# Preparations of passes one to three among the second pass's first products, and logits' products in pairs

## The chip, the cores and the metric

The kernel runs on one core of one Trainium2 chip. The metric is the device time of one execution in microseconds. Three runs of the kernel before took 724.37, 722.12 and 724.14 us, a median of 724.14. Each core has a matrix engine (TensorE, PE in the profile, its weight loads PEld), VectorE (DVE), ScalarE (ACT), GpSimd (POOL), and a sequencer (SP) that here issues most of the transfers. Each engine runs its own instructions in the order in which they were laid down.

## The reference, cut to what matters

One decoder layer on 512 tokens of width 1024: token mixing (attention and gated DeltaNet branches), whose merged result `m` goes through an output projection, and then a mixture of 32 experts in 4 groups of 8.

```python
h = rms_norm(x, norm1_w) * (1 + sc1) + sh1
x = x + g1 * (m @ w_out)                        # output projection
h = rms_norm(x, norm2_w) * (1 + sc2) + sh2
pg = softmax(h @ w_rg + b_rg)                   # group logits: 4
le = (h @ w_re + b_re).reshape(T, 4, 8)         # expert logits: 32
# the best group, in it the best 2 experts; comb = their weights
for e in range(32):
    a = silu(h @ w_gate[e]) * (h @ w_up[e])     # 1024 -> 256, twice
    y = y + (a * comb[:, e]) @ w_down[e]        # 256 -> 1024
out = rms_norm(x + g2 * y, final_norm_w)
```

Every token goes through two experts only. All data are float32.

## The kernel before, in words

**The output projection** (`project_out`, from about 413 us). The 1024 output features stand in 8 blocks of 128, features on the partitions, the 512 tokens along the row. Block i takes 24 matrix products, three for each of 8 slices k (`mm3`, lines 138 to 140: float32 split into a high and a low part). VectorE then adds the gated sum to the residual stream (line 1058, `x1 = blk(i)`). While the blocks run, the 36 routing logits (32 experts, 4 groups) are summed up too: two blocks at a time, behind blocks 1, 3 and 5, two products (line 1078) with 64 weight columns each, the even block into output partitions 0 to 63 of one accumulator bank, the odd one into 64 to 127. Four transposes for each block (`rows`, line 1050) turn the finished blocks to token rows, ScalarE copies these back (line 1051), and the first half of the rows is stored to DRAM (`xd`) by a transfer that ScalarE issues (line 1090); the second half follows behind the projection. ScalarE and VectorE split the next block's weights meanwhile (lines 143, 144).

**The experts** (`moe`, from about 477 us). 13 passes handle 128 token places each: passes 0 to 9 hold two experts (64 and 64 places, or 96 and 32), passes 10 to 12 four experts of 32. Passes 0 to 2 hold six experts that are fixed beforehand; for the later ones VectorE ranks the experts by their token counts, so their weights can be asked for only when that order is known. A pass needs these steps:

- `match(p)`: VectorE compares the tokens' positions with a counter and so makes the one-hot table of tokens by places (line 1645).
- `places(p)`: 12 tiny products on TensorE turn the table into the token numbers (`idx`) and a scale of each place. `weights(p)`: 4 tiny products more for the routing weights of the places (lines 1702, 1704). From pass 3 on `places` does both.
- `fetch(p)`: GpSimd issues an indirect transfer that gathers the 128 rows from `xd` (line 1683).
- `scale(p)`: ScalarE scales the left half of the rows, VectorE the right half (lines 1708, 1709).
- `features(p, b)`: four transposes (line 1718) of half b; ScalarE (b = 0, line 1722) or VectorE (b = 1, line 1725) copies them, modulated, into `xe`. Pass 0 has another way (`first_rows`): products with a one-hot table straight from the blocks, and no gather.
- `up(p)`: 8 blocks k of products of `xe` with the gate and up weights (line 1796), each expert in its own group of output partitions; then silu (line 1818), `gate` on VectorE (line 1823), `turn` (two transposes, line 1831, and ScalarE's copy, line 1832), and `down(p)` (line 1847), which VectorE and ScalarE evacuate (lines 1858 to 1861).
- `add(n)`: 8 pairs of products scatter the pass's result back to the token rows, one pass later (lines 1870 to 1872).

**The order.** `step` ties the first TensorE and SP instructions of a part behind the last ones of the part before, so on TensorE and SP the written order holds. What isn't tied is placed by a planner with its own costs. `tc.issue_after(x)` adds such a tie: instructions inside the block come behind x on x's engine, without a wait between engines. `between` of `up` is called ahead of each block k: in pass 0 `first_steps` puts the work on the routing there: at k = 0 the features of pass 0 and places and gathers of passes 1 and 2, at k = 2 the ranks of the tokens and the tables of routing weights, at k = 4 `match(0)` and `places(0)`, at k = 7 `weights(0)`. Behind `up(0)` stand `scale(1)`, `gate(0)`, `features(1, 0)`, `features(1, 1)`, `turn(0)` and `down(0)`, one load, and then `weights(1)`, `weights(2)`, `match(3)`, `places(3)` and `fetch(3)`, before `up(1)` begins.

**The weights' stream.** The experts' weights, 96 units of 1 MB (two for up and one for down of each expert), go through a ring of 18 tiles. SP asks for the next units behind blocks 3 and 7 of `up` and behind `down` (`load`, line 1005), each request waiting until the products that read the tile before are done.

The code around the change, with the lines of the profile:

Of the kernel before, what the change touches and what calls it, by code (L numbers as in the profile page):

```python
# [34 lines left out]
NP = len(PASSES)  # L35
# [22 lines left out]
def rows(p):  # L58
    o = 0
    for g, (q, n) in enumerate(p):  # L60
        yield g, q, slice(o, o + n)
        o += n
# [31 lines left out]
class Prog:  # L94
# [912 lines left out]
    def project_out(self):  # L1007
# [3 lines left out]
        with tc.tile_pool(name="ps_out", bufs=1, space=PSUM, reuse_waits="tile") as pp:  # L1011
# [34 lines left out]
            def rows(i):  # L1046

                p = pp.tile([128, 4, 128], F32, name="tr", bufs=2)
                for t in range(4):
                    nc.tensor.transpose(p[:, t], blk(i)[:, t], self.ident)  # L1050
                nc.scalar.activation(blk(i), p, AF.Copy)
            for i in range(7):
                wh, wl = self.unit_w(None, self.wo[i])
                ps = pp.tile([128, 512], F32, name="pj", bufs=2)
                for k in range(8):
                    self.mm3(ps, wh[:, k], wl[:, k], self.mhi[:, k], self.mlo[:, k], k == 0, k == 7)
                x1 = blk(i)
                v.scalar_tensor_tensor(x1, tiles(ps), self.mod[:, 16 + i:17 + i], x1, op0=OP.mult, op1=OP.add)
                if i == 0:
                    nc.scalar.activation(asq, x1, AF.Square)  # L1060
                else:
                    s2 = tiles(pp.tile([128, 512], F32, name="tr", bufs=2))
                    nc.scalar.activation(s2, x1, AF.Square)
                    v.tensor_add(asq, asq, s2)
                if i == 0:
                    with tc.issue_after(self.un_dma.ins):
                        nc.sync.dma_start(self.acc[:, :, 512:], I["xA"][:, :, 512:])
                        for j in (6, 7):
                            self.wo.append(self.uraw[j % 2])
                            self.un_dma = nc.sync.dma_start(self.wo[j], I["w_out"][:, j])  # L1070
                    with tc.issue_after(self.un_dma.ins):
                        self.load(12)
                elif i in (1, 3, 5):
                    self.load(1)
                if i in (1, 3, 5):

                    for g in range(2):
                        mm(tiles(lt[64 * g:64 * g + 64]), w6[:, i - 1 + g], blk(i - 1 + g), start=i == 1, stop=i == 5)
                    if i == 5:
                        nc.scalar.activation(lT, tiles(lt), AF.Copy)  # L1080
                elif i == 6:
                    pr[0] = pp.tile([128, 512], F32, name="rt0")[:, 0:36]
                    for t in range(4):
                        mm(pr[t], lT[:, t], sel, start=True, stop=False)
                        mm(pr[t], x1[:, t], self.wr[:, 6], start=False, stop=False)
                if i in (1, 3):
                    rows(i - 1)
                    rows(i)
                if i == 3:
                    nc.scalar.dma_start(xv[:, :, 0:512], self.acc[:, :, 0:512])  # L1090
                if i == 6:
                    psq = pp.tile([128, 512], F32, name="tr", bufs=2)
                    for t in range(4):
                        sums(psq[:, t:t + 1], asq, t)
                    v.tensor_scalar(ss, psq[:, 0:4], 1.0 / D, EPS, op0=OP.mult, op1=OP.add)
# [262 lines left out]
    def moe(self, es):  # L1358
# [32 lines left out]
        for p in range(NP):  # L1391
            if 0 < p < NP - 1:
                with ExitStack() as late:
                    for x in self.after_down:
                        late.enter_context(tc.issue_after(x))
                    self.scale(p + 1)
            if 0 < p < NP - 3:
                self.match(p + 3)
            if p == NP - 1:
                self.step(self.finish_init)  # L1400
                with ExitStack() as late:
                    for x in self.after_down:
                        late.enter_context(tc.issue_after(x))
                    self.step(self.alike, p)
            self.up(p, between=self.first_steps if p == 0 else None)
            if p == 0:
                with tc.issue_after(self.at_tables):
                    self.scale(1)
            self.gate(p)
            if p + 1 < NP:  # L1410
                self.step(self.features, p + 1, 0)
                if p == 0:
                    self.step(self.features, 1, 1)
            else:
                self.step(self.gather, 1)
            if p:
# [29 lines left out]
                    self.step(self.finish_last, h)  # L1446
                self.store_last(p)
            self.step(self.load, len(PASSES[p]) - (p == 0))
            if p == 0:
                for i in (1, 2):  # L1450
                    self.step(self.weights, i)
                self.match(3)
                self.step(self.places, 3)
                self.fetch(3)
        self.last = {}
        self.rest()

# [301 lines left out]
    def first_steps(self, k):  # L1759
# [12 lines left out]
        elif k == 2:  # L1772
            self.step(self.by_rank)
            self.tables()

            with self.tc.issue_after(self.at_exp):
                self.nc.scalar.activation(self.nt2[:, 0:1], self.ones[:, 0:1], AF.Silu)
        elif k == 4:
            self.match(0)
            self.step(self.places, 0)  # L1780
        elif k == 7:
            self.step(self.weights, 0)

    def up(self, p, experts=None, part=None, between=None):

# [150 lines left out]
```

## Time and profile before

| what | value |
|---|---|
| profiled execution, device time | 724.38 us |
| its span, first to last instruction | 722.5 us |
| TensorE busy | 692.8 us (96%) |
| VectorE busy | 485.5 us (67%) |
| ScalarE busy | 283.0 us (39%) |
| experts' weights into tiles `ra`, `rb`: median from issue to landing | 10.6 and 10.7 us |
| mean granted TensorE clock | 0.993 of full |

A busy TensorE isn't TensorE at its peak, as products are pipelined and their ends are modelled; starts are to be trusted more than durations. The granted clock is the share of full speed that the chip let TensorE have in a stretch. The DMA share is the mean busy share of the core's 16 DMA engines. In the rows on the timeline a number in brackets is the time that the engine stood idle before the instruction, and the arrow names what ended the wait. Lines L138 to L1872 are lines of the kernel.

### The profile page before, as it was taken

The numbers are of one execution on the slowest core, as the hardware profiler recorded it, in microseconds if no ns is written. First come the engines' busy times: TensorE is split into PE (matmuls) and PEld (weight loads), VectorE is DVE, ScalarE is ACT, GpSimd is POOL, SyncE is SP. The second block draws the span as 40 slices with busy tenths as digits, with TensorE's granted clock in tenths as the row PEclk, the third lists the DMA queues.
The fourth block names the chain that finished last, engine by engine and source line by source line (L and its number), as shares of the span: only waits on it lengthen the run. The fifth ranks groups of instructions, "written<-read, shape, count | busy, mean of one in ns | idle before, by whom it ended". The sixth has DMA issues, their size and how long they took to land. (4 is left out here: it accounts for less than half of the span.)

```text
span 722.5 us, 10988 instructions
## 1 busy us (share of the span) xinstructions
PE 692.8 (96%) x3939; PEld 481.7 (67%) x3939; DVE 485.5 (67%) x1243; ACT 283.0 (39%) x554; POOL 36.1 (5%) x43
## 2 busy tenths in 40 slices
PE   7999999999999899999999999998899999999995
PEld 5887868878798777876778867793444444554531
DVE  6987669968447677578766744284577766777654
ACT  5745357652233224367652323143122222322352
POOL 0002000520000000000000000100000000000000
PEclk9999999999999999999999999999999999999998
DMA  9942221058765772361168998068799999999994
GB/s 357 394 168 69 97 85 62 30 149 295 215 235 191 250 251 89 120 232 60 44 215 282 340 422 354 2 237 322 277 351 418 418 415 404 419 417 418 427 418 190
DMA packets 47756, 183.12 MB, mean 253 GB/s; under 512 B 11786, under 2 KB 12330, under 8 KB 34514
## 3 DMA queue, kind: packets, MB, share of 16 engines
q1 hardware_dynamic: 40930, 169.65, 62.3%
q10 hardware_dynamic: 4896, 8.51, 3.3%
q0 software_dynamic: 1872, 4.23, 1.6%
q8 instruction: 32, 0.52, 0.3%
q14 instruction: 26, 0.21, 0.1%
HBM read 175.63 MB, written 9.33 MB: 256 GB/s over the span
## 5 line engine op out<-in xcount | busy, mean ns | idle before, releaser
L138 PE MATMUL pj<-hR,uR 128*128 128x512 f32 x304 | 122.3, 402 | 1.5 <-DVE qk L762 1.5
L140 PE MATMUL pj<-hR,uS 128*128 128x512 f32 x304 | 122.1, 402 | 0.0
L139 PE MATMUL pj<-hR,uR 128*128 128x512 f32 x304 | 122.0, 401 | 0.0
L143 ACT ACTIVATE uR<-uF 128x1024 fp32r<-128x1024 f32 x48 | 50.8, 1060 | 104.1 <-PE pj L139 97.3
L1796 PE MATMUL gu<-ra,uS 128*64 128x512 f32 (+1 forms) x368 | 85.0, 604 | 1.4 <-DMA ra<-w_e 1.4
L144 DVE TENSOR_TENSOR uS<-uF,uR 128x1024 fp32r<-128x1024 f32 x48 | 58.4, 1219 | 25.8 <-ACT uR L143 24.1
L138 PEld LDWEIGHTS pj<-hR,uR 128*128 128x128 f32 x304 | 57.3, 188 | 14.2 <-issue 1.9
L140 PEld LDWEIGHTS pj<-hR,uS 128*128 128x128 f32 x304 | 57.3, 188 | 12.5 <-DVE uS L144 0.4
L139 PEld LDWEIGHTS pj<-hR,uR 128*128 128x128 f32 x304 | 57.3, 188 | 11.9 <-issue 0.3
L1872 DVE TENSOR_TENSOR accF<-accF,cb 128x512 f32<-128x512 f32 x96 | 59.7, 680 | 6.3 <-PE cb L1871 5.4
L219 DVE SCALAR_TENSOR_TENSOR sgF<-sgF,misc 128x1024 f32<-128x1024 f32 x32 | 38.9, 1218 | 12.7 <-DMA sgF<-w_mod 12.7
L1796 PEld LDWEIGHTS gu<-ra,uS 128*64 128x64 f32 (+1 forms) x368 | 25.0, 125 | 32.5 <-issue 27.8
L1823 DVE SCALAR_TENSOR_TENSOR uS<-uS,meta,gu 128x256 f32<-128x256 f32 x13 | 6.2, 480 | 55.1 <-ACT uS L1818 55.1
L1860 ACT ACTIVATE uR<-p2F 128x512 fp32r<-128x512 f32 x24 | 15.1, 632 | 67.2 <-DVE p2F L1858 63.3
L1870 PE MATMUL cb<-uR,oht 128*128 128x512 f32 x96 | 40.0, 416 | 0.0
L1871 PE MATMUL cb<-uR,oht 128*128 128x512 f32 x96 | 37.9, 395 | 0.0
L1796 PE MATMUL gu<-rb,uS 128*32 128x512 f32 (+1 forms) x136 | 32.5, 593 | 0.0
L1818 ACT ACTIVATE uS<-gu 128x256 f32<-128x256 f32 x13 | 5.0, 384 | 64.9 <-PE gu L1796 64.9
L138 PE MATMUL pj<-mR,uR 128*128 128x512 f32 (+1 forms) x72 | 27.3, 379 | 0.0
L409 DVE SCALAR_TENSOR_TENSOR dF<-dF,c_cols 128x512 f32<-128x512 f32 x36 | 26.6, 748 | 0.9
L139 PE MATMUL pj<-mR,uR 128*128 128x512 f32 (+1 forms) x72 | 27.0, 375 | 0.0
L140 PE MATMUL pj<-mR,uS 128*128 128x512 f32 (+1 forms) x72 | 26.8, 372 | 0.0
(437 smaller groups left out, 1346.0 us busy)
## 6 DMA issues: line engine op xcount, KB each, us to landing
ra<-w_e SPq DMA_DIRECT2D x54, 1024.0 KB, 10.6
rb<-w_e SPq DMA_DIRECT2D x25, 1024.0 KB, 10.7
uF<-w_in SPq DMA_DIRECT2D x38, 512.0 KB, 3.3
sgF<-w_mod SPq DMA_DIRECT2D x32, 512.0 KB, 4.8
rc<-w_e SPq DMA_DIRECT2D x15, 1024.0 KB, 8.1
sF<-w_mod SPq DMA_DIRECT2D x8, 1024.0 KB, 9.0
gd<-sgF ACTq DMA_DIRECT2D x16, 256.0 KB, 2.8
gF<-gd SPq DMA_DIRECT2D x8, 512.0 KB, 4.5
```

The source lines that it names most:

```text
L138: mm(ps, whi, xhi, start=first, stop=False)
L139: mm(ps, whi, xlo, start=False, stop=False)
L140: mm(ps, wlo, xhi, start=False, stop=last)
L143: self.nc.scalar.activation(hi, raw, AF.Copy)
L144: self.nc.vector.tensor_sub(lo, raw, hi.bitcast(F32))
L219: self.nc.vector.scalar_tensor_tensor(raw, raw, 1.0, self.cact, op0=OP.mult, op1=OP.mult, accum_out=self.mod[:, ot:ot + 1])
L409: nc.vector.scalar_tensor_tensor(a, r[:, k:k + 512], w[:, k:k + 1], a, op0=OP.mult, op1=OP.add)
L1796: nc.tensor.matmul(gu[r], xe[:, k, r], w[:, k % 4], start=k == 0, stop=k == 7)
L1860: i1 = nc.scalar.activation(self.yhi[:, c], self.yf[:, c], AF.Copy)
L1870: nc.tensor.matmul(pc, self.oht[:, ts], self.yhi[:, c], start=True, stop=False)
L1871: nc.tensor.matmul(pc, self.oht[:, ts], self.ylo[:, c], start=False, stop=True)
L1872: nc.vector.tensor_add(self.acc[:, t, c], self.acc[:, t, c], pc)
```

## The change

In the projection, the two logits' products of a pair, the transposes of the two blocks, and behind the last pair the copy of the logits, now stand in a helper `pair`. It is called inside blocks 2, 4 and 6, ahead of slice k = 2, and ties the two products one behind the other and behind the products of slice 1, and those of slice 2 behind both. In the experts, `weights(0)` moves from k = 7 to k = 4 of `up(0)`; `scale(1)` and `features(1, 0)` move from behind `up(0)` to its k = 6; `weights(1)`, `weights(2)` and `match(3)` move from the end of pass 0 to k = 3 of `up(1)`, `places(3)` and `fetch(3)` to its k = 5, and `match(4)` from ahead of `up(1)` to behind `fetch(3)`.

```diff
@@ -1049,11 +1049,29 @@
                 for t in range(4):
                     nc.tensor.transpose(p[:, t], blk(i)[:, t], self.ident)
                 nc.scalar.activation(blk(i), p, AF.Copy)
+            def pair(i):
+
+                w = next(x for x in reversed(nc.cur_bb.bb.instructions) if x.engine == mybir.EngineType.PE)
+                for g in range(2):
+                    with tc.issue_after(w):
+                        w = mm(tiles(lt[64 * g:64 * g + 64]), w6[:, i + g], blk(i + g), start=i == 0, stop=i == 4).ins
+                if i == 4:
+                    nc.scalar.activation(lT, tiles(lt), AF.Copy)
+                else:
+                    with tc.issue_after(w):
+                        rows(i)
+                        rows(i + 1)
+                    if i == 2:
+                        nc.scalar.dma_start(xv[:, :, 0:512], self.acc[:, :, 0:512])
+                return w
             for i in range(7):
                 wh, wl = self.unit_w(None, self.wo[i])
                 ps = pp.tile([128, 512], F32, name="pj", bufs=2)
                 for k in range(8):
-                    self.mm3(ps, wh[:, k], wl[:, k], self.mhi[:, k], self.mlo[:, k], k == 0, k == 7)
+                    with ExitStack() as es:
+                        if k == 2 and i in (2, 4, 6):
+                            es.enter_context(tc.issue_after(pair(i - 2)))
+                        self.mm3(ps, wh[:, k], wl[:, k], self.mhi[:, k], self.mlo[:, k], k == 0, k == 7)
                 x1 = blk(i)
                 v.scalar_tensor_tensor(x1, tiles(ps), self.mod[:, 16 + i:17 + i], x1, op0=OP.mult, op1=OP.add)
                 if i == 0:
@@ -1072,22 +1090,11 @@
                         self.load(12)
                 elif i in (1, 3, 5):
                     self.load(1)
-                if i in (1, 3, 5):
-
-                    for g in range(2):
-                        mm(tiles(lt[64 * g:64 * g + 64]), w6[:, i - 1 + g], blk(i - 1 + g), start=i == 1, stop=i == 5)
-                    if i == 5:
-                        nc.scalar.activation(lT, tiles(lt), AF.Copy)
-                elif i == 6:
+                if i == 6:
                     pr[0] = pp.tile([128, 512], F32, name="rt0")[:, 0:36]
                     for t in range(4):
                         mm(pr[t], lT[:, t], sel, start=True, stop=False)
                         mm(pr[t], x1[:, t], self.wr[:, 6], start=False, stop=False)
-                if i in (1, 3):
-                    rows(i - 1)
-                    rows(i)
-                if i == 3:
-                    nc.scalar.dma_start(xv[:, :, 0:512], self.acc[:, :, 0:512])
                 if i == 6:
                     psq = pp.tile([128, 512], F32, name="tr", bufs=2)
                     for t in range(4):
@@ -1394,7 +1401,7 @@
                     for x in self.after_down:
                         late.enter_context(tc.issue_after(x))
                     self.scale(p + 1)
-            if 0 < p < NP - 3:
+            if 1 < p < NP - 3:
                 self.match(p + 3)
             if p == NP - 1:
                 self.step(self.finish_init)
@@ -1402,15 +1409,10 @@
                     for x in self.after_down:
                         late.enter_context(tc.issue_after(x))
                     self.step(self.alike, p)
-            self.up(p, between=self.first_steps if p == 0 else None)
-            if p == 0:
-                with tc.issue_after(self.at_tables):
-                    self.scale(1)
+            self.up(p, between=self.first_steps if p == 0 else self.second_steps if p == 1 else None)
             self.gate(p)
             if p + 1 < NP:
-                self.step(self.features, p + 1, 0)
-                if p == 0:
-                    self.step(self.features, 1, 1)
+                self.step(self.features, p + 1, int(p == 0))
             else:
                 self.step(self.gather, 1)
             if p:
@@ -1446,12 +1448,6 @@
                     self.step(self.finish_last, h)
                 self.store_last(p)
             self.step(self.load, len(PASSES[p]) - (p == 0))
-            if p == 0:
-                for i in (1, 2):
-                    self.step(self.weights, i)
-                self.match(3)
-                self.step(self.places, 3)
-                self.fetch(3)
         self.last = {}
         self.rest()
 
@@ -1778,8 +1774,22 @@
         elif k == 4:
             self.match(0)
             self.step(self.places, 0)
-        elif k == 7:
             self.step(self.weights, 0)
+        elif k == 6:
+            with self.tc.issue_after(self.at_tables):
+                self.scale(1)
+            self.step(self.features, 1, 0)
+
+    def second_steps(self, k):
+
+        if k == 3:
+            for i in (1, 2):
+                self.step(self.weights, i)
+            self.match(3)
+        elif k == 5:
+            self.step(self.places, 3)
+            self.fetch(3)
+            self.match(4)
 
     def up(self, p, experts=None, part=None, between=None):
 
```

## Rows read from the trace of the kernel before

**Rows 1.** The page's first part: busy time, share of the span and number of instructions of each engine.

```profile
PE 692.8 (96%) x3939; PEld 481.7 (67%) x3939; DVE 485.5 (67%) x1243; ACT 283.0 (39%) x554; POOL 36.1 (5%) x43
```

**Rows 2.** Busy time by stretch of the expert passes: the stretch from and to (us), its length, then busy time and number of instructions of PE, PEld, DVE, ACT and POOL, the granted TensorE clock, the DMA share and GB/s.

```profile
493.00:500.00 7.00, 6.04 (x40) 2.46 (x38) 3.43 (x11) 2.84 (x7) 0.00 (x0) 1.00 0.80 302
500.00:507.00 7.00, 3.94 (x24) 1.32 (x24) 3.81 (x11) 1.92 (x4) 0.00 (x0) 1.00 1.00 358
507.00:513.00 6.00, 5.75 (x34) 2.15 (x36) 2.48 (x10) 0.00 (x0) 0.99 (x1) 0.72 0.52 173
513.00:520.00 7.00, 7.00 (x54) 3.88 (x51) 2.78 (x7) 1.97 (x6) 0.00 (x0) 1.00 0.84 286
520.00:527.00 7.00, 6.00 (x30) 3.06 (x30) 6.92 (x31) 0.31 (x1) 0.99 (x1) 1.00 0.92 365
527.00:534.00 7.00, 7.00 (x35) 2.71 (x32) 3.28 (x6) 2.02 (x4) 0.00 (x0) 1.00 0.83 286
534.00:640.00 106.00, 106.00 (x704) 50.97 (x704) 76.39 (x177) 28.52 (x63) 6.92 (x7) 1.00 1.01 416
```

**Rows 3.** TensorE's timeline (start, duration, engine, line, operation, out<-in, shape, count): the turn of pass 2, the turn of pass 11, and, in up of the last pass, the fourth expert's first product.

```profile
536.49 0.42 PE L1831 MATMUL gu<-ct,uS 128*128 128x128 f32 x2
...
679.76 0.38 PE L1831 MATMUL gu<-ct,uS 128*128 128x128 f32 x2
...
688.71 0.62 PE L1796 MATMUL gu<-ra,uS 128*32 128x512 f32 x1 [1.42 <-DMA ra<-w_e]
```

**Rows 4.** TensorE's timeline around the first pair of logits' products, at the start of block 2 of the projection.

```profile
425.39 0.40 PE L139 MATMUL pj<-mR,uR 128*128 128x512 f32 x1
425.63 0.40 PE L140 MATMUL pj<-mR,uS 128*128 128x512 f32 x1
425.95 1.07 PE L1078 MATMUL rt<-accF,oF 128*64 128x512 f32 x2
426.96 0.50 PE L138 MATMUL pj<-mR,uR 128*128 128x512 f32 x1
427.39 1.07 PE L1078 MATMUL rt<-accF,oF 128*64 128x512 f32 x2
428.39 0.66 PE L1050 MATMUL tr<-ct,accF 128*128 128x128 f32 x4
```

**Rows 5.** TensorE's timeline over down of pass 0, first and last products, and the weights' products behind them.

```profile
500.10 0.64 PE L1847 MATMUL cb<-uR,uS 128*64 128x512 f32 x1 [1.06 <-ACT uS L1832]
500.10 0.64 PE L1847 MATMUL cb<-ra,uS 128*64 128x512 f32 x1
500.58 0.59 PE L1847 MATMUL cb<-uR,uS 128*64 128x512 f32 x1
...
503.15 0.59 PE L1847 MATMUL cb<-uR,uS 128*64 128x512 f32 x1
...
503.68 0.35 PE L1702 MATMUL tr<-p2F,uS 128*128 128x6 bf16 x8
```

**Rows 6.** VectorE's timeline: the sum of block 1 of the projection.

```profile
426.06 0.75 DVE L1058 SCALAR_TENSOR_TENSOR accF<-pj,mod,accF 128x512 f32<-128x512 f32 x1 [3.46 <-PE pj L140]
```

**Rows 7.** TensorE's timeline from block 7 of up of pass 0 to the end of up of pass 1 (down of pass 0 left out).

```profile
496.50 1.08 PE L1796 MATMUL gu<-ra,uS 128*64 128x512 f32 x4
497.51 1.09 PE L1718 MATMUL tr<-ct,uF 128*128 128x128 f32 x8
498.60 0.44 PE L1831 MATMUL gu<-ct,uS 128*128 128x128 f32 x2
...
507.25 0.35 PE L1670 MATMUL tr<-MC,uS 128*128 128x1 bf16 x8 [3.22 <-DVE uS L1645]
...
507.74 5.35 PE L1796 MATMUL gu<-ra,uS 128*64 128x512 f32 x16
512.92 3.60 PE L1796 MATMUL gu<-rb,uS 128*64 128x512 f32 x16
516.46 0.65 PE L1718 MATMUL tr<-ct,uF 128*128 128x128 f32 x4
```

**Rows 8.** The timelines of VectorE and of ScalarE from the tables of routing weights to the match of pass 3.

```profile
489.85 0.28 DVE L1325 CAST p2F<-p2F 128x128 bf16<-128x128 f32 x1
...
493.12 0.72 ACT L1708 ACTIVATE uF<-uF,meta 128x512 f32<-128x512 f32 x1 [3.24 <-DMA uF<-xd,idx]
...
499.65 0.40 ACT L1832 ACTIVATE uS<-gu 128x256 f32<-128x256 f32 x1
...
498.64 1.37 DVE L1725 TENSOR_SCALAR uS<-tr,A,mod 128x128 f32<-128x128 f32 x4
...
505.21 0.69 DVE L1861 TENSOR_TENSOR uR<-p2F,uR 128x512 fp32r<-128x512 f32 x1
505.92 0.51 DVE L1704 TENSOR_REDUCE meta<-tr 64x1 f32<-64x3 f32 x3
506.44 0.76 DVE L1645 TENSOR_TENSOR uS<-ct,p2F 128x384 bf16<-128x384 f32 x2
```

**Rows 9.** SP's timeline: the requests behind block 3 of up of pass 1 and behind down of pass 1; and of the line that issues the gathers, the time from issue to landing of all twelve.

```profile
513.12 1.50 SPq L1005 DMA_DIRECT2D ra<-w_e  x2
...
526.91 1.59 SPq L1005 DMA_DIRECT2D rb<-w_e  x2
...
DMA to landing us min/median/max: 3.9/7.7/8.2
```

## The prediction

> **What bounds the kernel now.** The page's first part shows TensorE busy for 96% of the span [rows 1]; since a busy share can hide a wait for weights, the second view is the table of stretches over the expert passes [rows 2]. It shows two limits side by side: from 534 to 640 us TensorE is busy in all of 106.00 us, and the DMA engines are at share 1.01 with 416 GB/s. The transposes of the gated activations (L1831) of passes 2 and 11 start at 536.49 and 679.76, so nine passes take 143.27 us, 15.92 each, with no gap on TensorE. The last pass then waits 1.42 us for its weights [rows 3]. So TensorE's order sets the passes' pace, freed ring tiles set when weights may be asked for, and the stream of weights is never idle after 534; the end moves earlier by what TensorE gains before that, if the stream loses idle time too. It has idle time to lose: (1 - share) times length over the stretches from 493 to 534 gives 1.4 + 0 + 2.9 + 1.1 + 0.6 + 1.2 = 7.2 us [rows 2]. The chain of waits on the page ends in the last store and says nothing here. What the change can win is therefore read from TensorE's timeline: the output projection [rows 4] and the step from pass 0 to pass 1 [rows 7].
>
> **Part 1, the pairs of logits' products.** Ordinary output products start 0.23 us apart (425.39, 425.63). Then a logits' product of block 0 starts at 425.95, one output product (L138) at 426.96, the logits' product of block 1 at 427.39, and the transposes at 428.39 [rows 4]: 1.00, 0.43 and 1.00, in all 2.44 us. These logits' products fill 64 output columns each, one the lower and one the upper half, like the experts' products of two experts. The down products of pass 0 show what such neighbours cost: both start at 500.10, the second passes at 500.58, and from the last two (503.15) to the next work is 0.53 [rows 5]. Two of them together take 0.48 + 0.53 = 1.01 us, as long as one takes here alone, because the two halves run at once. The pair so costs 1.01 and the displaced output product its ordinary 0.23: 2.44 - 1.24 = 1.20 us saved, and 3 pairs give 3.6 us. TensorE has no gap between the ordinary products around it, so this is all on the path.
>
> Bounds: if the halves did not overlap, each would keep its 1.00 and only the broken-in product's extra 0.20 would go: 0.6 us for three. A loss needs the new fixed place to come before the block's sum is ready: VectorE writes it from 426.06 to 426.81 [rows 6], and the pair is due behind six products of the block that starts about 425.86, at 427.3, so 0.5 us of slack; the same cadence holds for the later pairs. Above, 1.3 per pair. I take 3.6, as rows 5 are the same tile shape and row length. The transposes to rows, their copies, the copy of the logits and the first store keep their number; they come 1.4 us later in a block of 5.6, and ScalarE, which issues that store, is not waited for there. Everything behind the projection hangs on TensorE's products, so the 3.6 us carry to the passes.
>
> **Part 2, from pass 0 to pass 1.** Now down of pass 0 ends at 503.68, small weights' products follow, TensorE waits 3.22 us for VectorE's match of pass 3, runs the places at 507.25, and needs 507.74 to 512.92 = 5.18 us for the first four blocks of pass 1's up products and 512.92 to 516.46 = 3.54 for the other four [rows 7]. The granted clock was 0.72 in that stretch against 1.00 before and after [rows 2]: full speed lost for part of it, after the gap; that cost 5.18 - 3.54 = 1.64. From 503.68 to 516.46 are 12.78 us. After the change pass 1's blocks follow down directly and the preparations stand among them: 2 x 3.54 = 7.08; weights' products 0.35 [rows 5]; places 507.25 to 507.74 = 0.49; and four more changes between 64-column and full products at 0.10 each, 0.40: the last step of down took 0.53 where a block of 3.54 / 4 = 0.885 is two ordinary steps of 0.44. Sum 8.32, gain 4.46.
>
> The match is hidden only if VectorE is done with it before block 5. VectorE ends down's evacuation at 505.90; the weights' products stand behind block 2, at about 503.9 + 3 x 0.885 = 506.5; four reductions (three took 0.51 at 505.92, so 0.7) and the match (0.76 at 506.44) give 508.0 [rows 8]; the places are due at 506.5 + 0.45 + 1.77 = 508.7. Cover 0.7 us; if it is missed, TensorE waits the difference, at most the 3.22 of today, and blocks 5 to 7 and the loads behind them wait with it. The match of pass 4 comes behind it on VectorE, which then stands nearly idle until the gate. Bounds of part 2: 4.46 - 1.64 if the clock still falls, 1.2 if also half of today's wait stays, and 5.0 if the changes of shape cost nothing and a little of the 1.06 us before down goes.
>
> The Trainium skill, "TensorEngine Tiling (Array Packing)", section Key Properties, speaks against this part: changing the tiling mode drains the engine, and the change puts full-width work between 64-column products at two new places. No page price is needed: by the rows that is the 0.40 already in the sum, and without it the gain would be 4.86.
>
> **Part 3, the tail of pass 0.** Four of the eight feature transposes (1.09 for eight, so 0.54) move in front of block 6, with two changes of shape (0.2): up ends 0.74 later. They need ScalarE's scaling, which waited for the gathered rows until 493.12 and was done at 493.84 [rows 8]; block 6 starts about 496.50 - 0.88 = 495.6 [rows 7], a cover of 1.8 us. ScalarE's four feature copies are then done under blocks 6 and 7, so the copy at 499.65, which stood behind them, can follow the turn (498.60, 0.44 long) at once: 0.55 won. Net loss 0.2; up to 0.34 more (a quarter of the 1.37 at 498.64) if VectorE takes a feature in front of the gate. The weights of pass 0, three blocks earlier, need tables done at 490.13 [rows 8], well before block 4. The two loads behind block 7 come 0.7 later, while 1.4 us of DMA idle time lies around them.
>
> **Queues.** On SP the two loads now at 513.12 follow block 3 of pass 1: 503.9 + 0.35 + 4 x 0.885, about 507.8, 5.3 earlier; those at 526.91 come 4.3 earlier [rows 9]. Between them lie four 1 MB loads and now two gathers instead of one: at 416 GB/s 5.2 MB take 12.6 us, inside the 14.8, so the stream keeps up and later stays full as today. On POOL the gather for pass 3 goes out near 509.5 as now, but behind two loads; gathers landed within 8.2 us [rows 9], so by 518, even if the queue is longer by a load (2.5) by 520.5, before its scaling is due after down of pass 1 (about 522).
>
> **The sum.** 3.6 + 4.46 - 0.2 = 7.9 us. The profiled execution took 724.38, its span 722.5 and 1.88 around it; the median shown is 724.14, 0.24 below. 724.38 - 7.9 = 716.5, and 0.24 less as a median: **716.2**.
>
> **Rivals.** (1) The halves do not overlap, because the logits' products share one accumulator bank: 0.6 instead of 3.6, so 719.2. For it, the trace shows no logits' pair side by side; against it, the experts' products also share one bank by halves and overlap. (2) The clock still falls in pass 1, or the match is late: 1.64 to 2.5 less, 717.9 to 718.7. For it, the 1.06 us gap before down stays [rows 5], and TensorE's light work from 480 on is unchanged; against it, the clock was at 1.00 through that gap and fell only after the 3.22 us. The Trainium skill, "TensorE: Matmul & The Clock Gate", section Part 1, says the half clock is the default state, which recent activity releases; by that rule the fall after the wait is expected, and a fall without it is not excluded. (3) More comes back: the stream also loses the idle time behind 526, and the 1.06 us gap shrinks: 10 us, 714.1. (4) Slower: TensorE takes its work in order, so the transposes in front of block 6 hold blocks 6, 7 and the loads behind them until the gather for pass 1 has landed. It landed about 493.0; the stall begins when it lands 1.8 us later, and eats the whole 7.9 only 9.7 us later, at 502.7. Gathers landed 3.9 to 8.2 us after their issue [rows 9], so even from the quickest to the slowest are 4.3 us, a stall of 2.5; past 9.7 the price would be 724 to 728. (5) The change doesn't do it: the planner still parts the pairs, or fills pass 1's start with the preparations: within 1 us of now.
>
> **How the numbers follow.** Forecast 0.60 (own range 714.8 to 717.6), rival 1 0.10, rival 2 0.13, rival 3 0.07, rival 4 0.04, rival 5 0.06. A measurement tells about 0.3% from no change, 2.2 us. Faster: 0.60 + 0.10 + 0.13 + 0.07 = 0.90; same 0.06; slower 0.04. The range reaches from 713.6, inside rival 3, to 720.4, past rival 1 with the weaker bound of part 2.
>
> **What would show it.** Right: each logits' pair on TensorE starts its two products within 0.02 us and takes about 1.0; no wait for VectorE's match between down of pass 0 and pass 1; granted clock 1.00 there; pass 1's up about 8.3 us long; the last pass's wait for weights still there, some 8 us earlier. Wrong: a wait in front of block 6, logits' products one after the other, a drop of the clock in pass 1, or DMA idle time after 530.

## The result, and the profile after

The changed kernel takes **716.28 us** (median; 715.83 to 717.32) against 724.14: ratio 0.99, 95% interval 0.9879 to 0.992. The forecast was 716.2. The profiled execution took 716.23, its span 714.3, which is 8.2 less than the 722.5 of before. One execution of a kernel below (e6) took 1750.48 us and is left out of its ratio.

The page's first part is the counterpart of [rows 1]:

```profile
PE 685.9 (96%) x3939; PEld 479.6 (67%) x3939; DVE 485.9 (68%) x1243; ACT 283.3 (40%) x554; POOL 36.2 (5%) x43
```

The same 3939 instructions keep TensorE busy for 6.9 us less, and the share is still 96%: it says nothing of where the time went. The stretches do. These answer to [rows 2], moved by seven or eight microseconds (same columns: stretch, length, busy time and count of PE, PEld, DVE, ACT and POOL, granted clock, DMA share, GB/s):

```profile
486.00:493.00 7.00, 7.00 (x54) 2.56 (x50) 1.86 (x7) 1.29 (x4) 0.90 (x1) 1.00 0.74 246
493.00:500.00 7.00, 6.08 (x30) 2.12 (x28) 2.56 (x7) 1.88 (x6) 0.00 (x0) 1.00 1.01 414
500.00:507.00 7.00, 7.00 (x54) 2.57 (x52) 5.57 (x18) 1.73 (x3) 0.57 (x1) 1.00 0.88 317
507.00:513.00 6.00, 6.00 (x47) 4.14 (x44) 4.50 (x17) 2.28 (x6) 0.42 (x1) 1.00 1.01 422
513.00:520.00 7.00, 5.99 (x31) 2.55 (x31) 6.97 (x24) 1.18 (x3) 0.99 (x1) 1.00 0.76 284
520.00:526.00 6.00, 6.00 (x31) 2.68 (x28) 2.01 (x4) 1.34 (x4) 0.00 (x0) 1.00 0.98 411
526.00:632.00 106.00, 106.00 (x703) 50.53 (x703) 76.72 (x177) 28.40 (x62) 6.94 (x7) 1.00 1.01 413
```

Nothing is left of the stretch at clock 0.72 with 3.94 busy in 7 us ahead of it; the clock is 1.00 throughout. The idle time of the DMA engines, (1 - share) times length, falls from 7.2 to 1.8 + 0.8 + 1.7 + 0.1 = 4.4 us, and the long stretch of the passes looks as before. TensorE's timeline shows the edited places, first the projection [rows 4], then pass 0 to pass 1 [rows 5, 7], then the last passes [rows 3]. Its columns are start, duration, engine, line, operation, out<-in, shape and count, and in brackets the wait ahead and what ended it:

```profile
413.29 0.40 PE L138 MATMUL pj<-mR,uR 128*128 128x512 f32 x1
...
427.14 1.08 PE L1057 MATMUL rt<-accF,oF 128*64 128x512 f32 x4
428.15 0.66 PE L1050 MATMUL tr<-ct,accF 128*128 128x128 f32 x4
...
491.70 0.66 PE L1714 MATMUL tr<-ct,uF 128*128 128x128 f32 x4
492.29 1.94 PE L1806 MATMUL gu<-ra,uS 128*64 128x512 f32 x8
494.16 0.66 PE L1714 MATMUL tr<-ct,uF 128*128 128x128 f32 x4
495.25 0.44 PE L1841 MATMUL gu<-ct,uS 128*128 128x128 f32 x2 [0.44 <-DVE uS L1833]
496.17 0.64 PE L1857 MATMUL cb<-uR,uS 128*64 128x512 f32 x1 [0.47 <-ACT uS L1842]
...
499.65 2.75 PE L1806 MATMUL gu<-ra,uS 128*64 128x512 f32 x12
502.33 0.35 PE L1698 MATMUL tr<-p2F,uS 128*128 128x6 bf16 x8
502.61 1.08 PE L1806 MATMUL gu<-ra,uS 128*64 128x512 f32 x4
503.52 1.03 PE L1806 MATMUL gu<-rb,uS 128*64 128x512 f32 x4
504.48 0.35 PE L1666 MATMUL tr<-MC,uS 128*128 128x1 bf16 x8
...
504.97 2.80 PE L1806 MATMUL gu<-rb,uS 128*64 128x512 f32 x12
507.69 0.66 PE L1714 MATMUL tr<-ct,uF 128*128 128x128 f32 x4
...
514.50 3.65 PE L1857 MATMUL cb<-rb,uS 128*64 128x512 f32 x16 [1.01 <-issue]
...
670.99 0.38 PE L1841 MATMUL gu<-ct,uS 128*128 128x128 f32 x2
678.75 1.04 PE L1806 MATMUL gu<-ra,uS 128*32 128x512 f32 x2 [0.24 <-DMA ra<-w_e]
681.24 0.62 PE L1806 MATMUL gu<-ra,uS 128*32 128x512 f32 x1 [1.45 <-DMA ra<-w_e]
...
700.35 3.67 PE L1857 MATMUL cb<-ra,uS 128*32 128x512 f32 x32 [0.47 <-ACT uS L1842]
703.95 1.98 PE L1507 MATMUL cb<-p2F,rb 128*128 128x512 f32 x4
```

The reader is to see five things. The logits' products now stand as one group of four ahead of the transposes and take 1.01 us (427.14 to 428.15), with no output product inside. The match of pass 3 no longer releases anything: the places (L1666) start at 504.48 with no wait in front of them. Block 6 (492.29) starts right behind the moved transposes, with no wait for the gather. The wait before down (1.06 in [rows 5]) is now two short ones, 0.44 before the turn and 0.47 before down. And in the last pass a wait for weights remains.

From run to run the first output product moves by a few microseconds (411 to 417 us in the kernels below; 413.29 and 414.64 in two profiles of the changed kernel), which has nothing to do with the edits, as nothing ahead of it was changed. The device times hold this spread too. So the tables from here on count from that product (413.50 before, 413.29 after). The columns: the product that counts the routed tokens (L1249, now L1256), the first product of down of pass 0, the end of up of pass 1, the turn of pass 11, the end of the span.

```
                   count   down of 0   up of 1 ends   turn of 11     end
before             65.55     86.60       102.96         266.26     309.01
after              61.90     82.88        94.40         257.70     301.06
gained so far       3.65      3.72         8.56           8.56       7.95
```

### The profile page after: what moved, and what is told of

Same layout as the page of the kernel before. It is cut to its first block, busy times and chain, and to the rows that moved or that the text cites. A ratio compares the mean times of both kernels' runs of the same rounds, so it can differ in the third digit from the quotient of the medians.

```text
span 714.3 us, 10991 instructions
## 1 busy us (share of the span) xinstructions
PE 685.9 (96%) x3939; PEld 479.6 (67%) x3939; DVE 485.9 (68%) x1243; ACT 283.3 (40%) x554; POOL 36.2 (5%) x43
```

## The experiments

**Each part alone.** The first kernel has the pairs of the change and everything from the routing on as before; the second has the reverse.

```diff
 e1_pairs_only (on the changed kernel)
-            self.up(p, between=self.first_steps if p == 0 else self.second_steps if p == 1 else None)
+            self.up(p, between=self.first_steps if p == 0 else None)
...
+            if p == 0:
+                for i in (1, 2):
+                    self.step(self.weights, i)
+                self.match(3)
+                self.step(self.places, 3)
+                self.fetch(3)
...
-        elif k == 6:
-            with self.tc.issue_after(self.at_tables):
-                self.scale(1)
-            self.step(self.features, 1, 0)
...
```

> The projection as changed, the expert passes as before. My theory (the two halves of a pair run at once, 1.2 us saved for each of three pairs, and all that follows starts earlier by that): about 3.6 us faster than before, 720.5, and every turn of pass 0 to 11 about 3.6 earlier. Rival A (the weights' stream sets the end, so a gain of TensorE ahead of the passes is given back while it waits for weights): under 1.5 us faster, 723 or more, with the wait for weights in the last pass grown by 2 us or more.

> The projection as before, the expert passes as changed. My theory: up of pass 1 takes about 8.1 us from the end of down of pass 0 with no wait and the clock at full, 4.7 us gained there, and the end 4.1 to 4.7 earlier, 719.4 to 720. With the pairs alone this adds up to the whole change (7.9). Rival A (stream sets the end): under 2 us faster. Rival B (the two parts share a gain, as each fills the same idle time of the stream): each alone gives 5 us or more, the sum more than 9.

Measured: pairs alone 720.38, ratio 0.996 (0.994 to 0.9979); steps alone 718.42, ratio 0.9928 (0.9912 to 0.9944), with 723.51 before. So 3.1 and 5.1 us, together 8.2, where the whole change gives 7.9: the parts add up, and each is there without the other. To the end of the span the profiles give 2.70 and 5.28. At the turn of pass 11 they give 2.45 and 4.87, 1.2 less than the 8.56 of both together; the pairs alone lost nearly all of that to the clock, as follows.

The count comes at 61.91 with the pairs alone, the full 3.64 earlier. But up of pass 1 ends only 2.45 earlier (at 512.73, which is 100.51 behind the first output product at 412.22). TensorE's timeline of the pairs alone shows why:

```profile
502.34 0.37 PE L1677 MATMUL tr<-MC,uS 128*128 128x1 bf16 x8 [3.22 <-DVE uS L1652]
...
502.86 6.50 PE L1803 MATMUL gu<-ra,uS 128*64 128x512 f32 x16
509.20 3.60 PE L1803 MATMUL gu<-rb,uS 128*64 128x512 f32 x16
```

and the stretch of these blocks:

```profile
500.00:508.00 8.00, 5.66 (x28) 1.99 (x30) 4.49 (x17) 0.87 (x2) 0.99 (x1) 0.61 0.63 225
```

The wait for the match is again 3.22, but the four blocks behind it take 509.20 - 502.86 = 6.34 us, where the kernel before took 5.18 [rows 7]; the last four take 3.53, as there (3.54). Cut into pieces of 1 us, the granted clock is 0.50, the lower of its two levels (1.2 GHz), from 502 to 508 us here, and in the kernel before only from 509 to 511, with 0.58 and 0.71 in the pieces beside. So the same steps behind the same wait paid 1.64 us in one kernel and 2.80 (6.34 - 3.54) in the other. What made the low clock last longer here, these runs don't show; a kernel that keeps the wait keeps that spread.

**Are the halves of the pair what saves the 3.6 us?** Rival 1 said they don't overlap. Two kernels take the overlap away, each in another way: one puts both products on the lower 64 output columns, the other lets an output product of full width stand between them.

```diff
 e3_same_half
...
-                        w = mm(tiles(lt[64 * g:64 * g + 64]), w6[:, i + g], blk(i + g), start=i == 0, stop=i == 4).ins
+                        w = mm(tiles(lt[0:64]), w6[:, i + g], blk(i + g), start=i + g == 0, stop=i + g == 5).ins
...
 e8_split_pair
+                    if g == 0:
+                        with tc.issue_after(w):
+                            w = mm(ps, wh[:, 2], self.mhi[:, 2], start=False, stop=False).ins
...
+                        if k == 2 and i in (2, 4, 6):
+                            mm(ps, wh[:, k], self.mlo[:, k], start=False, stop=False)
+                            mm(ps, wl[:, k], self.mhi[:, k], start=False, stop=False)
...
```

> The changed kernel, but both products of a logits' pair go into the lower half of the output partitions, one after the other, at the same fixed place; the sums are added up there. My theory (the halves running at once is the gain): a pair takes 1.9 to 2.0 us instead of 1.0, three of them 2.7 to 3.0 us later than the changed kernel, about 719.1. Rival C (the gain is the fixed place, and that no output product breaks in between): as the changed kernel, 716.3, within 0.6.

> The changed kernel with the first output product of slice 2 between the two products of each logits' pair, at the same fixed place. My theory (only neighbours run at once): each pair and that product take 2.4 us again instead of 1.24, three of them 3.6 us, about 719.9. Rival C (the fixed place is the gain): within 0.6 of 716.3.

Measured: 718.95, ratio 0.9936 (0.9917 to 0.9954), with the same half, beside 723.51 before; 717.62, ratio 0.9908 (0.9872 to 0.9943), with the pair split, beside 723.77 before. The second time misses the 719.9 that was expected, and by itself it would not rule out rival C; TensorE's timeline decides. With the same half:

```profile
430.62 1.93 PE L1057 MATMUL rt<-accF,oF 128*64 128x512 f32 x4
432.48 0.77 PE L1050 MATMUL tr<-ct,accF 128*128 128x128 f32 x5
```

and with the pair split:

```profile
426.30 1.07 PE L1057 MATMUL rt<-accF,oF 128*64 128x512 f32 x2
427.30 0.50 PE L1060 MATMUL pj<-mR,uR 128*128 128x512 f32 x1
427.74 1.07 PE L1057 MATMUL rt<-accF,oF 128*64 128x512 f32 x2
428.74 0.66 PE L1050 MATMUL tr<-ct,accF 128*128 128x128 f32 x4
```

The same four instructions (two for each product) take 1.86 us on one half and 1.01 on two. The split pair takes 428.74 - 426.30 = 2.44 with the product inside it, to the hundredth what before took [rows 4], and the count comes at 65.48, as before (65.55); the turn of pass 11 is 3.73 later than in the changed kernel. With the same half the count comes at 64.78 (481.55 - 416.77). So of the 3.65 us, 64.78 - 61.90 = 2.88 are the overlap of the two column halves, and it needs the two products to be neighbours in TensorE's order. The other 65.55 - 64.78 = 0.77 come without overlap, as no output product breaks into the pair any more; rival 1 worked out 0.6 for that.

**The wait or the clock?** In the kernel before, idle products (nothing reads what they make; eleven of them, two instructions each) fill TensorE's wait for the match, and nothing else is changed.

```diff
 e4_gap_filled (on the kernel before)
                 self.match(3)
+                self.step(self.warm, self.gu.tile([128, 512], F32, name="gu"), self.ident, 11)
                 self.step(self.places, 3)
```

> The kernel before, with eleven idle products of 128 columns (some 2.8 us) laid into TensorE's wait for the match of pass 3. My theory (the wait makes the clock fall, and that costs 1.64 us of the 4.7): the granted clock stays 1.00 in pass 1, the first four blocks of up take 3.5 us instead of 5.2, and the end comes about 1.5 us earlier, 722.6. Rival D (the clock falls in pass 1 because of the light work ahead of it, gap or not): clock and time as before, 724.1.

Measured: 722.79 against 723.51, ratio 0.9982 (0.996 to 1.0003), which the times alone can't tell from no change. TensorE's timeline can:

```profile
503.13 2.70 PE L214 MATMUL gu<-ct 128*128 128x128 f32 x22
506.49 0.35 PE L1671 MATMUL tr<-MC,uS 128*128 128x1 bf16 x8 [0.66 <-DVE uS L1646]
...
506.97 3.65 PE L1797 MATMUL gu<-ra,uS 128*64 128x512 f32 x16
510.46 3.60 PE L1797 MATMUL gu<-rb,uS 128*64 128x512 f32 x16
```

and the stretch:

```profile
506.00:512.00 6.00, 5.51 (x40) 2.24 (x42) 2.71 (x11) 0.00 (x0) 0.99 (x1) 1.00 0.60 193
```

The match still ends the wait, so nothing of the 3.22 is won. But the clock stays at 1.00, the first four blocks take 510.46 - 506.97 = 3.49 instead of 5.18, and up of pass 1 ends 1.70 earlier (101.26). That is the 1.64 that the prediction had put down to the clock, shown by itself: the light work ahead of the wait is unchanged, so rival D is refuted, and the gain is still there at the turn of pass 11 (264.57 for 266.26). The Trainium skill, "TensorE: Matmul & The Clock Gate", section Part 1, calls the half clock the default, which activity releases; the filled wait, with the clock at 1.00, agrees.

**The moved feature transposes.** Four of them back behind block 7, all else as changed:

```diff
 e6_features_behind
             self.gate(p)
             if p + 1 < NP:
-                self.step(self.features, p + 1, int(p == 0))
+                self.step(self.features, p + 1, 0)
+                if p == 0:
+                    self.step(self.features, 1, 1)
...
-            self.step(self.features, 1, 0)
```

> The changed kernel, but the first half of pass 1's features stands behind up of pass 0 again, as before. By the prediction's part 3 (moving them costs 0.2 us): down of pass 0 starts 0.2 us earlier against the first output product than in the changed kernel. Rival F (moving them wins time, as ScalarE is free for the turned activations): down starts up to 0.2 us later. Either way the time stays within 0.5 us of 716.3.

Measured: 715.74, ratio 0.9894 (0.9858 to 0.993). TensorE around the turn of pass 0:

```profile
495.38 0.44 PE L1842 MATMUL gu<-ct,uS 128*128 128x128 f32 x2
496.87 0.64 PE L1858 MATMUL cb<-uR,uS 128*64 128x512 f32 x1 [1.05 <-ACT uS L1843]
```

The 1.05 us wait of [rows 5] is back, and the turn has no wait; down starts at 496.87 - 413.94 = 82.93 against 82.88. Moving the transposes wins as much as it costs.

**Does TensorE or the stream of weights set the end?** From 526 us on both are full. Six idle products ahead of pass 6 make TensorE later in the middle of the passes:

```diff
 e5_delay_pass6
+            if p == 6:
+                self.step(self.warm, self.bank(), self.ident, 6)
             self.up(p, between=self.first_steps if p == 0 else self.second_steps if p == 1 else None)
```

> The changed kernel with six idle products of 128 columns (about 1.5 us) on TensorE ahead of pass 6. My theory for the rest of the gain (TensorE came 8.8 us earlier to the last pass, the weights for it only 7.3, so the stream sets the end there): the waits for weights in the last pass (0.24 and 1.45 us) shrink to about 0.2 in all, the last pass's turn keeps its place against the first output product within 0.3 us, and the time stays at 716.3. Rival E (TensorE's order sets the end, and the weights follow it): the waits keep their length and the end comes 1.5 us later.

```profile
670.65 0.38 PE L1843 MATMUL gu<-ct,uS 128*128 128x128 f32 x2
...
679.10 0.62 PE L1808 MATMUL gu<-ra,uS 128*32 128x512 f32 x1 [0.92 <-DMA ra<-w_e]
```

Measured: 715.94, ratio 0.9893 (0.9857 to 0.9928), which is no different from the change. The turn of pass 11 comes 1.85 later (259.55), so the delay took hold. The wait for the fourth expert's weights shrinks only from 1.45 to 0.92, and the span ends 0.95 later than in the changed kernel's first profile. So the waits did not shrink to the 0.2 that was expected with the stream as the limit, nor did they keep their length. One profile's end does not tell which of the two sets the end; the profiles of all kernels whose last pass is the same do. In order of the turn of pass 11, counted as above:

```
                        turn of 11     end     between
before                    266.26     309.01     42.75
gap filled, e4            264.57     306.98     42.41
pairs only, e1            263.81     306.31     42.50
pair split, e8            261.43     303.83     42.40
steps only, e2            261.39     303.73     42.34
same half, e3             260.69     302.92     42.23
delay, e5                 259.55     302.01     42.46
features behind, e6       257.76     300.02     42.26
changed again, e9         257.72     300.00     42.28
changed                   257.70     301.06     43.36
```

The turns lie 8.56 us apart, and in all but one profile the end follows within 42.2 to 42.8 us: the end follows TensorE. The stream of weights, whose ring tiles TensorE's products free, follows it too: the fourth expert's first product, which waits for its weights in each of these kernels, comes 8.45 to 9.40 us behind the turn, whenever that is. Only the changed kernel's first profile stands out (10.25 and 43.36); why its weights landed a microsecond later stays open. Against its second, the delay comes out at the end in full (2.01 later, with the turn 1.83 later). The times, with the spread of the first output product in them, don't show it.

**The 1.0 us that is left before down of pass 1.** That wait (1.01, put down to "issue") was there in the kernel before as well:

```profile
523.26 3.65 PE L1847 MATMUL cb<-rb,uS 128*64 128x512 f32 x16 [1.00 <-issue]
```

It follows the overflow's steps, by which VectorE, fed by four small products, works out which experts have more tokens than their places; they stand behind the gate of pass 1, and here ahead of block 2 of pass 2's up. The edited kernel was run twice, the second time beside the changed kernel itself.

```diff
 e7_overflow_later, e10_overflow_again
-                if p == 1:
-                    self.overflow()
-                    self.off = self.free
-                    self.rest_init()
...
+    def third_steps(self, k):
+        if k == 2:
+            self.step(self.overflow)
+            self.off = self.free
+            self.rest_init()
```

> The changed kernel with the count of the tokens left over, 16 short VectorE operations in pass 1's tail, moved to block 2 of pass 2's up products. My theory (the 1.0 us that TensorE still waits before down of pass 1 is VectorE being late with the sums that free the accumulator banks): the wait goes, down of pass 1 starts 1.0 us earlier, its two loads too, the stream loses that much idle time, and the end comes 0.7 to 1.0 us earlier, 715.4. Rival G (the wait is for something else, or the stream gives it back): the wait or the end stays, 716.3.

> The changed kernel once more, as the measure for the two beside it. The last pass's wait for weights differed between runs by up to 1 us with the same MB moved, so what is read here is the spread: the time 715 to 717.5, the turn of pass 11 257.7 us behind the first output product, and the wait for weights in the last pass anywhere from 0.9 to 1.7.

> The kernel with the count of left-over tokens in pass 2 once more, beside the changed one on the same chip. My theory (VectorE's lateness cost TensorE 1.0 us ahead of down of pass 1, and the stream follows TensorE): the turn of pass 11 is 1.0 us earlier against the first output product, and the median 0.8 to 1.2 below that of the changed kernel. Rival G (the stream gives it back): the turn is earlier, the median within 0.4.

TensorE in the second of the two, e10:

```profile
512.06 0.60 PE L1710 MATMUL tr<-ct,uF 128*128 128x128 f32 x4
512.59 1.08 PE L1860 MATMUL cb<-rb,uS 128*64 128x512 f32 x4
```

```
                     down of 1   turn of 11     end
changed                101.22      257.70     301.06
changed again, e9      101.22      257.72     300.00
overflow later, e7      99.83      256.68     298.99
the same again, e10     99.97      256.81     298.94
```

Down of pass 1 follows the transposes at once. VectorE's timeline of the changed kernel shows what it had waited for, the fifth of the eight sums that scatter the result of pass 0. It reads an accumulator `cb`, and down writes into such accumulators:

```profile
513.72 0.68 DVE L1882 TENSOR_TENSOR accF<-accF,cb 128x512 f32<-128x512 f32 x1
```

It ends at 514.40, 0.10 us before down (514.50), and 0.10 is the distance in all ten profiles in which the overflow's steps stand ahead of it on VectorE; without them it ends 0.64 before down. So the wait ends with VectorE's sum, though the trace names no releaser; that it is for the accumulator is the likely reading, as the trace does not number them. TensorE is 1.3 to 1.4 us earlier there and 0.9 to 1.0 at the turn of pass 11. By times: 716.03, ratio 0.9889 (0.986 to 0.9919), no different from the changed kernel; and in the second run 714.41, ratio 0.9846 (0.9816 to 0.9876), beside 717.17, ratio 0.9886 (0.9854 to 0.9917), for the changed kernel. The intervals overlap, so the gain is shown in TensorE's order and only likely in the time. The first two lines of the table are one and the same kernel: equal to 0.02 us up to the turn of pass 11, and 1.06 apart at the end. A difference of one microsecond between two single profiles' ends is therefore nothing to build on.

**Sums of the last pass earlier.** On top of that, the eight additions that stand behind block 3 of the last pass's up move ahead of block 0, where TensorE waited for weights.

```diff
 e11_adds_first (on e7_overflow_later)
+            if p == NP - 1 and k == 0:
+                for n in (0, 2, 4, 6, 1, 3, 5, 7):
+                    self.step(self.add, n)
...
-                    for n in range(8):
-                        self.step(self.add, n)
```

> As the one before, and in the last pass the eight sums of pass 11's results stand ahead of block 0 of up instead of behind block 3. My theory (TensorE comes to the last pass before its weights, and can do that 4 us of work while they land): the waits for weights at block 0 go, a shorter wait appears ahead of block 4 or in down, where the last weights land, and the end comes 0.5 to 1.7 us earlier than without. Rival H (the sums need the evacuation of down of pass 11, so TensorE waits for VectorE instead): the wait changes its name, and the end stays within 0.4 or comes later.

```profile
679.01 0.49 PE L1884 MATMUL cb<-uR,oht 128*128 128x512 f32 x1 [0.42 <-ACT uR L1874]
...
679.73 0.50 PE L1885 MATMUL cb<-uR,oht 128*128 128x512 f32 x1 [0.23 <-DVE uR L1875]
...
699.47 5.60 PE L1861 MATMUL cb<-ra,uS 128*32 128x512 f32 x32 [0.47 <-ACT uS L1846]
```

Measured: 716.16, ratio 0.9862 (0.9828 to 0.9895); no gain over e10. The long wait for weights is gone, and two short ones (0.42, 0.23), for ScalarE and VectorE as rival H had it, stand in its place; but down of the last pass now takes 5.60 instead of the 3.67 that it has in e10 and in the changed kernel. A load of TensorE's weights in it waits for a transfer, which none does in e10:

```profile
701.45 0.15 PEld L1861 LDWEIGHTS cb<-ra,uS 128*32 128x32 f32 x7 [0.33 <-DMA ra<-w_e]
```

The span ends 1.3 us later than in e10 (300.27 against 298.94). From the turn of pass 11 that is 43.35 us, no more than the changed kernel's first profile took (43.36), so this one profile shows no gain and does not prove a loss. What stretched it may be the stores of the output rows, which start 4.5 us earlier (275.24 behind the first output product instead of 279.71) and run beside the last weights: SP's timeline here

```profile
690.37 10.05 SPq L1496 DMA_DIRECT2D out<-ra  x4
```

and in e10

```profile
692.33 6.22 SPq L1496 DMA_DIRECT2D out<-ra  x4
```

That is argued from these two rows; no run holds the stores back by themselves, and the first profile of the changed kernel was as late with its stores at 281.82. What is shown is that the time won ahead of the wait for weights came back as a wait later in the same pass.

## Why the prediction was right

**Part 1, 3 x 1.20 = 3.6 us:** 3.65. The pair takes 1.01, as was read from the down products of pass 0 [rows 5]. The kernel with one half shows that 2.88 of it are the overlap, and the one with the split pair that all of it goes when the two products are not neighbours.

**Part 2, 12.78 to 8.32, gain 4.46:** from 499.65 to 507.69 are 8.04, gain 4.74. The 0.28 between are in the smallest terms: the eight blocks take 2.68 + 0.91 + 0.96 + 2.72 = 7.27 instead of 7.08, so the four changes between 64-column and full products cost 0.19 more than the 7.08 and not 0.40 more; and the weights' products took 0.28, not 0.35. The 7.08 had held one change too many: 3.54 for four blocks ends in a step of 0.53 in place of 0.43 (as down does in [rows 5]), and it was taken twice. The Trainium skill, "TensorEngine Tiling (Array Packing)", section Key Properties, has a change of tiling mode drain the engine; by these rows that is about (0.19 + 0.10) / 4 = 0.07 us a change here. The split into 3.22 for the wait and 1.64 for the clock, less what the new places cost, stands: e4 gave 1.70 for the clock alone. The cover of the match (0.7) held, as the places had no wait.

**Part 3, net loss 0.2:** a gain of 0.07. Up of pass 0 ended 0.51 later (0.74 forecast), and 0.58 came back before down (0.55 forecast). The forecast had counted two new changes of shape (0.2); but the weights' products of pass 0, which had broken in ahead of block 7, went to the places of pass 0 and took their two changes along. The transposes cost 0.59 (491.70 to 492.29), and 0.08 was saved there. So the term came out with the other sign, and e6 shows that it doesn't matter.

**Down of pass 0:** 0.10 more, since it ran 3.48 (496.17 to 499.65) instead of 3.58. Together 3.65 + 0.07 + 0.10 + 4.74 = 8.56 at the end of up of pass 1, against 7.9.

**To the end.** The 8.56 were kept whole for ten passes, to the turn of pass 11: the argument that TensorE's order sets the pace, and that the stream catches up, held. In the first profile the last pass then gave back 1.3, since the fourth expert's weights landed later: its first product is 7.26 earlier by the table's count, not 8.56. It won 0.7 in its down (from 700.35 to 703.95 are 3.60), which before ran from 707.82 to 712.11, 4.29:

```profile
707.82 4.36 PE L1847 MATMUL cb<-ra,uS 128*32 128x512 f32 x32 [0.47 <-ACT uS L1832]
712.11 1.98 PE L1511 MATMUL cb<-p2F,rb 128*128 128x512 f32 x4
```

The forecast had neither. In e9, the same kernel, only 0.23 was given back, and the span's end is 9.0 earlier than before. So that the sum of 7.9 met the 7.86 of the medians to 0.1 us is partly luck: it had 0.66 too little ahead of the last pass, and what the last pass adds or takes differs by 1 us between two profiles of one kernel.

**The rivals.** (1) is refuted by the trace, and e3 shows what it would have given. (2) is refuted by the clock of 1.00 and the missing wait; e1, where the wait is kept, shows its price. (3) came in part: the wait before down of pass 0 shrank, and the DMA engines' idle time behind 526 (1.2 us in [rows 2]) went too (0.1 in the stretch from 520), but the time did not come to 10 us less. (4) did not occur: block 6 had no wait in front of it. (5) is refuted by the order that TensorE shows.

## What to carry to other kernels

Two products that fill different column halves are worth being placed as direct neighbours: with one full-width product between them the whole overlap was lost here. A wait on TensorE can cost more than its length: where the clock falls behind it, the blocks that follow run slower, and the surplus is read as the same blocks' time before and after the clock is back. What TensorE won early here reached the end, some 42 us behind the turn of pass 11; the waits for weights of the last pass add a spread of 1 us, so one profile's end does not show a gain of that size.

## What the runs showed of the hardware that was not expected

Behind the same 3.22 us wait the first four blocks took 5.18 us in one kernel and 6.34 in another, and the stretch's clock was 0.72 and 0.61 (over stretches of 6 and 8 us). The two halves of a pair overlap wholly (1.01 for two against 1.86 on one half), but not across a single full-width product of 0.23. A wait of 1.0 us before down of pass 1 has no releaser in the trace ("issue"), and yet it ends 0.10 us behind a sum on VectorE in the ten profiles that have it and goes away when VectorE comes to that sum earlier. And in two profiles of one kernel, equal to 0.02 us up to the turn of pass 11, the first product with the last pass's fourth expert differed by 1.05 us (267.95 and 266.90) and the end by 1.06.
